# A two-layer decoder trunk: the instruction order worked out with the scheduler's timeline model in place of its default machine model

## The chip, the cores and the metric

The kernel runs on one core of a Trainium2 chip. The metric is the device time of one execution in microseconds (us); the time of a kernel is the median of its runs. The engines go by the names of the profile: PE (TensorE, matmuls), PEld (its weight loads), DVE (VectorE), ACT (ScalarE), POOL (GpSimd) and SP (SyncE, which issues the weight DMAs). Each engine works through its own list of instructions in the order in which they stand there, so the order decides which instruction stands behind which wait.

## The reference

256 tokens of 1024 features go through two layers. Cut to what matters here:

```python
x = x + mixer(rmsnorm(x))        # layer 0 ("even"): block attention (8 heads of 64) beside
                                 #   a Mamba-2 scan (16 heads), one input and one output projection
x = x + convffn(rmsnorm(x))      # 1024 -> 2816 gate and up, causal conv of width 3, 2816 -> 1024
x = x + ple(p[i], sigmoid(x))    # 256 -> 1024, gated
...                              # layer 1 ("odd"): the mixer is a gated DeltaNet, 16 value heads:
q, k, v = silu(causal_conv4(x @ w))
T = inv(I + strict_lower(beta * decay * k @ k.T))     # per head and chunk
o = norm(q @ state + intra_chunk(T, k, v)) * silu(z)  # z = x @ w_z
x = x + o @ w_out                # then the same FFN and per-layer embedding
```

Everything is float32.

## The kernel before, in words

**The matmul stream.** A float32 product is made of three matmuls on halves of 12 significant bits. `mm3` (L174) issues them for each of its k tiles at L181, L182 and L183; a tile over 1024 features is 8 k tiles, so 24 matmuls. This text calls one of these matmuls an mm3 instruction. The weights (about 140 MB) are streamed once, in blocks of 128 x 1024 by `piece` (L133): an SP DMA into one of 4 `raw` buffers, the high half `whi` on ACT (L155), the low half `wlo` on DVE (L156), into 4 buffers each. These two are placed at a priority 80 instructions ahead (L154).

**The layers.** `even` runs the attention and scan heads of layer 0 (decay rows through a DRAM round trip `rowdr` to the tile `AC`, L516, and the exponentials `E` from it, L529 to L532; the attention's sums of squares `sqk`, L563, and `pss`, L566). `ffn` and `ple` are long runs of mm3 work. `_odd` (L710) runs the DeltaNet over 8 head groups of two value heads. For each group there are

- `prep` (L785): two convolution tiles (`pgd`, 24 mm3 each), transposes `pkq` (L795), Gram matrices (L820, L821), and the inverse of four triangular 128 x 128 problems. That inverse is six levels, each `pY` on PE (L867), `zb` on DVE (L871), `pST` on PE (L875, L878), two copies on ACT; then two Newton steps, each `pR` on PE (L894 to L901), a copy on ACT (L903), `pC` on PE (L906), the update `S32` on DVE (L907).
- `vproj`: two `pgd` tiles for v and their transposes `pvT` (L920).
- `zproj` (L984): two tiles `pz` of 24 mm3 for the gate, whose results leave their bank on DVE (L991) into `z`, a tile of 4 buffers.
- `core` (L925): the chain `py0`, `pS1`, `pkS`, `X1` (DVE, L944), `py1`, `po`, then a norm of 13 small DVE instructions between ACT passes, and transposes `oT` (L981).
- `gate` (L996): reads `z`, writes the operands `gh` (L210) and `gl` (L211) of the output projection `w_out` (tiles `pwo`, L1005).

The loop at L1021 calls, for group kh: core(kh), gate(kh), prep(kh+2), vproj(kh+1), zproj(kh+2); `w_out` for the first half of the heads is called after the last group. PSUM banks of this phase: 3 shared by the `pgd`, `pz` and `pwo` tiles (chain `acc`), 1 for `core`, 2 and 1 for the two alternating `prep` chains.

**What sets the order.** The program above is only a list with priorities: earlier lines come first, the weight halves 80 ahead. The framework's scheduler plays the list in a simulated machine; whenever an engine of that machine is free, it takes the ready instruction of the highest priority, and the sequence of these choices becomes the order of each engine's list on the chip. Buffers are reused in the same rotation whatever the order. Which machine is simulated is set where the context is opened, at L1151.

Of the kernel before, what the change touches and what calls it, by code (L numbers as in the profile page):

```python
# [14 lines left out]
PSUM = bass.MemoryType.PSUM  # L15
# [16 lines left out]

# Columns of the packed per-feature vectors (feature on the partition).
PV = {}
# [6 lines left out]
NPV = _n  # L41
# Columns of the constants that depend on shapes alone.
CC = {}
# [7 lines left out]
class Trunk:  # L51
    def __init__(self, ctx, tc, stream, xT, pT, pv, tok, cst, out):
        self.tc, self.nc, self.ctx = tc, tc.nc, ctx
        self.stream, self.out = stream, out
        self.off = 0
        self.order = []
        self.n = 0
        self.pshare, self.share = 0.0, 0.0
        nc = self.nc
        ep = ctx.enter_context  # L60
        self.cpool = ep(tc.tile_pool(name="cpool", bufs=1))
        self.rawp = ep(tc.tile_pool(name="rawp", bufs=4))
        self.splp = ep(tc.tile_pool(name="splp", bufs=4))
        self.smallp = ep(tc.tile_pool(name="smallp", bufs=3))
        self.chain = ""
        self.nrm = ep(tc.tile_pool(name="nrm", bufs=1, space=PSUM))

        warm = self.cpool.tile([P, 1], F32, tag="warm", name="warm")
        nc.vector.memset(warm, 0.0)
        nc.scalar.activation(warm, warm, AF.Exp)  # L70
        # matmuls on zeros: TensorE's clock is up when the first operands arrive
        zt = self.cpool.tile([P, 256], F16, tag="zt", name="zt")
        nc.vector.memset(zt, 0.0)
        pz = self.nrm.tile([P, 512], F32, tag="nrm", name="pwarm")
        for _ in range(WARM):
            nc.tensor.matmul(pz[:, :T], zt[:, :P], zt, start=True, stop=True)
        self.pv = self.cpool.tile([P, NPV], F32, tag="pv", name="pv")
        nc.scalar.dma_start(self.pv, pv)
        xs = self.cpool.tile([P, KD, T], F32, tag="x", name="x")
        for m in range(0, KD, 2):  # L80
            nc.sync.dma_start(xs[:, m:m + 2], xT[:, m:m + 2])
        self.x = [xs[:, m] for m in range(KD)]
        self.tok = self.cpool.tile([P, 64], F32, tag="tok", name="tok")
        self.cst = self.cpool.tile([P, NCC], F32, tag="cst", name="cst")
        self.cst_src, self.tok_src = cst, tok
        self.pT = pT
        self.ones = self.cpool.tile([P, 1], F32, tag="ones", name="ones")
        nc.gpsimd.memset(self.ones, 1.0)
        self.ident = self.c("ident")
        self.id16 = self.cpool.tile([P, P], F16, tag="id16", name="id16")  # L90
        self.zb = [[self.cpool.tile([P, 4, P], F16, tag=f"zb{s}_{l}", name=f"zb{s}_{l}") for l in range(6)]
                   for s in range(1)]

# [1 line left out]
    def c(self, name):  # L95
# [11 lines left out]
    @contextmanager  # L107
    def psum(self, **banks):
        """The 8 PSUM banks of a phase, by the kind of work that rotates through them."""
        assert sum(banks.values()) <= 7  # L110
        with self.tc.tile_pool(name=self.uid("psum"), bufs=1, space=PSUM) as pool:
            self.psp, self.banks = pool, banks
            yield
# [12 lines left out]
    @contextmanager  # L126
    def on(self, chain):
        """Work of a chain of its own: its tiles don't wait for those of other chains."""
        was, self.chain = self.chain, chain
        yield  # L130
        self.chain = was

    def piece(self, blocks, lo=None):  # L133
        """Stream in weight blocks (array, layer, k0, nk, c0, nc), 1024 columns at a time, and split them."""
        nc = self.nc
        groups, g, cols = [], [], 0
        for b in blocks:
            n = b[3] * b[5]
# [27 lines left out]
    def lo_engine(self, share):  # L166
        """GpSimd takes a share of the low halves, VectorE the rest."""
        self.pshare += self.share if share is None else share
# [5 lines left out]
    def mm3(self, out, w, a, start=True, stop=True):  # L174
        """out += w.T @ a over k-tiles, w = (hi, lo) [128, nk, f], a = list of (hi, lo)."""
        nc = self.nc
# [26 lines left out]
    def split(self, src, hi, lo, scale=None):  # L203
        """hi + lo = src * scale, hi and lo of 12 significant bits."""
        nc = self.nc
# [7 lines left out]

# [1 line left out]
    def norm_begin(self, gain, pool=None):  # L215
# [42 lines left out]
    def replicate(self, r, n, dst=None):  # L258
        """[128 tok, n] -> [128, n*128] with row values on every partition."""
        nc = self.nc  # L260
# [7 lines left out]

# [1 line left out]
    def ffn(self, i, nxt):  # L270
# [38 lines left out]

# [1 line left out]
    def ple_proj(self, i, pool):  # L311
# [38 lines left out]

# [1 line left out]
    def conv4(self, pool, ps, w, b=None):  # L352
        """2 * silu(causal conv of R * ps), four taps, feature-major."""
        nc = self.nc
# [19 lines left out]
    def softplus(self, x, n, dst):  # L374
        """max(x, 0) + log1p(exp(-|x|)) on a [128, n] tile; log1p by its atanh series."""
        nc = self.nc
# [21 lines left out]
    def rowdram(self, col):  # L398
        """[128 tok, 32] -> [32, 128] in DRAM."""
        nc = self.nc  # L400
# [7 lines left out]

# [1 line left out]
    def even(self):  # L410
# [4 lines left out]
    def _even(self, mp):  # L415
# [5 lines left out]

        # dt, decay sums
        wdt, = self.piece([(W, 0, 0, KD, 4096, 16)])
# [42 lines left out]

        # B, C, x
        sw = lambda t: (lambda j: self.v("scw", t * 4 + j))
# [42 lines left out]
        def ssd(t):  # L511
            """heads 2t, 2t+1"""
            xf = feat[t]
# [26 lines left out]

        # q, k (feature-major), v (token-major)
        gqk = KEEP([P, 1], "gqk")
# [67 lines left out]

        # attention
        aA = []
# [42 lines left out]

        # z gate, group norm
        aS = []
# [29 lines left out]

        # output projection
        for m0 in (0, 4):
# [14 lines left out]

# [1 line left out]
    def odd(self):  # L706
# [3 lines left out]
    def _odd(self, mp):  # L710
# [16 lines left out]

        # beta, decay sums
        wab, = self.piece([(W, 0, 0, KD, 6144, 32)])
# [5 lines left out]
        for c in range(2):  # L735
            PE.transpose(ps[:, c * 32:(c + 1) * 32], abS[:, c * P:(c + 1) * P], ident[:32, :32])
        # softplus(a + dt_bias) and softplus(-b) = -log(sigmoid(b))
        ab = KEEP([P, 2, 32], "ab")
# [46 lines left out]
        def prep(kh):  # L785
# [17 lines left out]
            self.rsqrt(t, 4, rkq)  # L803
            # k stays as it is: 1 / |k| goes into the rows of the triangular system and its right sides,
            # and its solution times k needs none
            cs = TL([P, 3, 4], "cs", bufs=3)
# [8 lines left out]
            V.tensor_scalar(out=sq_, in0=rkq[:, 2:4], scalar1=128 ** -0.5, scalar2=None, op0=ALU.mult)  # L815
            # Gram matrices
            pk = self.sm("pkk")
# [7 lines left out]
            V.tensor_tensor(qk, pk[:, T:].rearrange("p (c t) -> p c t", c=2), bc(upper, 2), op=ALU.mult)  # L825
            # decays; index of a problem: chunk * 2 + head
            GC = KEEP([P, 4, P], "GC")
# [23 lines left out]
            Ll = TL([P, 4, P], "Ll", F16)  # L851
            # inverse of the unit triangular L by doubling its blocks; T16 = inv(L), S16 = its transpose
            T16 = TL([P, 4, P], "T16", F16)
# [34 lines left out]
            G.tensor_tensor(Ll, L32, L16, op=ALU.subtract)  # L888
            # two Newton steps in float32: S += S (I - L' S)
            S32 = TL([P, 4, P], "S32", bufs=3)  # L890
# [34 lines left out]
        def core(kh, st, bv):  # L925
            k2, qd, sq_, kt, Pm, S32, cs = st
            # chunk 0
            ps = self.sm("py0")
# [8 lines left out]
            A.activation(S1.rearrange("p e t -> p (e t)"), ps[:, :T], AF.Copy)  # L937
            # chunk 1
            ps = self.sm("pkS")
# [9 lines left out]
            A.activation(vn[1].rearrange("p e t -> p (e t)"), ps[:, :T], AF.Copy)  # L949
            # outputs, token-major, index of a problem: chunk * 2 + head  # L950
            po = self.sm("po")
            for e in range(2):
                PE.matmul(po[:, e * P:(e + 1) * P], Pm[:, e], vn[0][:, e], start=True, stop=True)
            for e in range(2):
                o = T + e * P
                PE.matmul(po[:, o:o + P], qd[:, e], S1[:, e], start=True, stop=False)
                PE.matmul(po[:, o:o + P], Pm[:, 2 + e], vn[1][:, e], start=False, stop=True)
            # normalisation over the value dim
            so = KEEP([P, 4, P], "so")
# [197 lines left out]
```

## Time and profile before

| | |
|---|---|
| median of 3 runs | 945.4 us (945.18 to 949.99) |
| profiled execution, span | 948.2 us |
| layer 0 mixer, 0 to 201 us | 201 us |
| layer 0 FFN and embedding, 201 to 417 us | 216 us |
| odd mixer, 417 to 730 us | 313 us |
| layer 1 FFN and embedding, 730 to 948 us | 218 us |

The profile is that of one execution, and its own time is its span of 948.2 us; no other time stands beside it. The stages are stretches of that span, with bounds where the tiles of one stage give way to those of the next. In each stretch the share of each engine's busy time shows which one has slack. Matmuls are pipelined and their ends are modelled, so the times between the starts of two PE instructions tell more than the busy time of one.

### The profile page before, as it was taken

What the parts mean: (1) busy time and instruction counts of PE and PEld (TensorE: products, weight loads), DVE (VectorE), ACT (ScalarE), POOL (GpSimd) and SP (SyncE); (2) the same over time, 40 slices, a digit from 0 to 9 for tenths busy, and PEclk for the clock granted to TensorE, in tenths of its full rate; (3) what the DMA queues carried; (4) which work ended last, traced back from release to release, by engine and by line L of the source; (5) the groups of instructions that cost most, each with busy time, mean ns of one, the idle gap of its engine ahead of it and who ended that gap; (6) DMA issues with size and microseconds to landing.
All of it is one profiled execution on the core that took longest, in us unless ns stands there. A gap on an engine that the chain in (4) does not pass through costs nothing.

```text
span 948.2 us, 19896 instructions
## 1 busy us (share of the span) xinstructions
PE 903.1 (95%) x7768; PEld 865.4 (91%) x7768; DVE 751.2 (79%) x1636; ACT 584.3 (62%) x1231; POOL 77.2 (8%) x83
## 2 busy tenths in 40 slices
PE   7979999999999999998989998999999999999998
PEld 5978778899999999987878898889899999999997
DVE  6767778888788766687889998999868888876665
ACT  5467656565655544664877777777745656654452
POOL 2000012110000001020111101111002000000100
PEclk9889999999999999999899999999999999999999
DMA  7544532456666555645333243322445555555562
GB/s 266 155 130 140 156 113 91 138 194 195 193 192 200 181 186 171 190 137 165 96 125 96 79 144 107 117 90 82 134 133 179 179 200 195 188 187 183 172 190 77
DMA packets 49822, 145.65 MB, mean 154 GB/s; under 512 B 9344, under 2 KB 15040, under 8 KB 49728
## 3 DMA queue, kind: packets, MB, share of 16 engines
q1 hardware_dynamic: 40608, 139.84, 46.7%
q10 hardware_dynamic: 9120, 4.53, 1.9%
q8 instruction: 61, 1.00, 0.4%
q14 instruction: 33, 0.27, 0.1%
HBM read 143.27 MB, written 1.08 MB: 152 GB/s over the span
## 4 chain that ended last, share of the span: by engine, by line
PE 75%; DVE 13%; DMA 4%; ACT 4%; issue 2%; POOL 1%; ACTq 0%; SPq 0%; POOLq 0%
PE pd L181 4%; PE pd L183 4%; PE pd L182 4%; PE pg L181 4%; PE pg L182 4%; PE pu L181 4%; PE pu L182 4%; PE pg L183 4%; PE pu L183 4%; DVE wlo L156 4%; DMA AC<-rowdr 2%; DMA GC<-rowdr 2%; PE pwo L182 2%; PE pgd L183 2%; PE pgd L181 2%
## 5 line engine op out<-in xcount | busy, mean ns | idle before, releaser
L156 DVE TENSOR_TENSOR wlo<-raw,whi 128x1024 fp32r<-128x1024 f32 (+2 forms) x266 | 323.5, 1217 | 89.1 <-ACT whi L155 85.6
L155 ACT ACTIVATE whi<-raw 128x1024 fp32r<-128x1024 f32 (+2 forms) x266 | 276.3, 1039 | 173.3 <-PE pd L182 46.3
L183 PE MATMUL pd<-yh,wlo 128*128 128x256 f32 x352 | 99.6, 283 | 0.0
L181 PE MATMUL pd<-yh,whi 128*128 128x256 f32 x352 | 99.6, 283 | 0.0
L182 PE MATMUL pd<-yl,whi 128*128 128x256 f32 x352 | 99.6, 283 | 0.0
L181 PE MATMUL pg<-xh,whi 128*128 128x256 f32 x352 | 97.3, 277 | 0.6 <-DVE x L1011 0.3
L181 PE MATMUL pu<-xh,whi 128*128 128x256 f32 x352 | 97.3, 277 | 0.0
L182 PE MATMUL pg<-xl,whi 128*128 128x256 f32 x352 | 97.3, 277 | 0.0
L183 PE MATMUL pg<-xh,wlo 128*128 128x256 f32 x352 | 97.2, 276 | 0.0
L182 PE MATMUL pu<-xl,whi 128*128 128x256 f32 x352 | 97.2, 276 | 0.0
L183 PE MATMUL pu<-xh,wlo 128*128 128x256 f32 x352 | 97.2, 276 | 0.0
L181 PE MATMUL pgd<-xh,whi 128*128 128x256 f32 x256 | 76.3, 298 | 0.3 <-DVE z L991 0.3
L182 PE MATMUL pgd<-xl,whi 128*128 128x256 f32 x256 | 74.9, 293 | 0.0
L183 PE MATMUL pgd<-xh,wlo 128*128 128x256 f32 x256 | 74.8, 292 | 0.0
L363 DVE SCALAR_TENSOR_TENSOR chh<-cg,pv,chh 128x255 f32<-128x255 f32 x132 | 66.7, 505 | 4.0 <-ACT chh L361 2.1
L183 PEld LDWEIGHTS pd<-yh,wlo 128*128 128x128 f32 x352 | 67.6, 192 | 0.0
L181 PEld LDWEIGHTS pd<-yh,whi 128*128 128x128 f32 x352 | 67.6, 192 | 0.0
L182 PEld LDWEIGHTS pd<-yl,whi 128*128 128x128 f32 x352 | 67.6, 192 | 0.0
L181 PEld LDWEIGHTS pg<-xh,whi 128*128 128x128 f32 x352 | 66.1, 188 | 0.8 <-issue 0.8
L182 PEld LDWEIGHTS pu<-xl,whi 128*128 128x128 f32 x352 | 66.1, 188 | 0.0
L183 PEld LDWEIGHTS pu<-xh,wlo 128*128 128x128 f32 x352 | 66.1, 188 | 0.0
L182 PEld LDWEIGHTS pg<-xl,whi 128*128 128x128 f32 x352 | 66.1, 188 | 0.0
(358 smaller groups left out, 2657.5 us busy)
## 6 DMA issues: line engine op xcount, KB each, us to landing
raw<-stream SPq DMA_DIRECT2D x232, 512.0 KB, 3.6
raw<-stream SPq DMA_DIRECT2D x32, 448.0 KB, 3.2
AC<-rowdr ACTq DMA_DIRECT2D x16, 128.0 KB, 4.0
GC<-rowdr ACTq DMA_DIRECT2D x16, 128.0 KB, 4.0
x<-xT SPq DMA_DIRECT2D x4, 256.0 KB, 5.0
out<-x SPq DMA_DIRECT2D x8, 128.0 KB, 1.8
cst<-cst SPq DMA_DIRECT2D x1, 645.0 KB, 6.4
raw<-pT SPq DMA_DIRECT2D x2, 256.0 KB, 2.5
```

Of the source, the lines that this page charges most:

```text
L155: nc.scalar.activation(hi[:, :cols], raw[:, :cols], AF.Copy)
L156: self.lo_engine(lo).tensor_tensor(lo_[:, :cols], raw[:, :cols], hi[:, :cols].bitcast(F32), op=ALU.subtract)
L181: nc.tensor.matmul(out, wh, ah, start=start and k == 0, stop=False)
L182: nc.tensor.matmul(out, wh, al, start=False, stop=False)
L183: nc.tensor.matmul(out, wl, ah, start=False, stop=stop and k == n - 1)
L363: nc.vector.scalar_tensor_tensor(out=h[:, s:], in0=g[:, :T - s], scalar=w(3 - s), in1=h[:, s:], op0=ALU.mult, op1=ALU.add)
```

## The change

The context is opened with the scheduler's timeline model as the simulated machine. Comments and docstrings were dropped as well; the line numbers stay.

```diff
-    with tile.TileContext(nc) as tc:
+    with tile.TileContext(nc, schedule_with_timeline_sim=True) as tc:
         order = tile_trunk(tc, **aps, out=out)
```

Both programs hold the same instructions on the same buffers on every engine. Only the order on each engine differs. Three places show how.

**ACT, layer 0, the first decay rows.** `E` needs `AC` from DRAM; `sqk` is what `pss` on PE waits for. Before:

```order
L516 DMA AC_158_741<-rowdr_88_335 128x256 x2
L516 DMA AC_164_767<-rowdr_88_335 128x256
L361 ACTIVATE chh_120_555<-cg_119_553,pv_106 128x256
L155 ACTIVATE whi_174_801<-raw_173_799 128x1024
L529 ACTIVATE E_162_750<-AC_158_741,ac_84_329 128x128
L530 ACTIVATE E_162_750<-AC_158_741,cross_90_339 128x128
L531 ACTIVATE E_162_750<-AC_158_741,ac_84_329 128x128
L529 ACTIVATE E_163_758<-AC_158_741,ac_84_329 128x128
L532 ACTIVATE E_162_750<-E_162_750 128x384
L560 ACTIVATE kT0_153_704<-pqk_152_679,gqk_128_580 128x256
L370 ACTIVATE cth_122_561<-chh_120_555 128x256
L563 ACTIVATE sqk_154_706<-pqk_152_679 128x256
```

With the change:

```order
L404 ACTIVATE rowsb_86_333<-rowps_85_331 32x128
L406 DMA rowdr_88_335<-rowsb_86_333 32x128
L560 ACTIVATE kT0_153_704<-pqk_152_679,gqk_128_580 128x256
L563 ACTIVATE sqk_154_706<-pqk_152_679 128x256
L155 ACTIVATE whi_187_879<-raw_186_877 128x1024
L370 ACTIVATE cth_122_561<-chh_120_555 128x256
L502 ACTIVATE gm0_124_567<-pG_123_564 128x128
L361 ACTIVATE chh_138_622<-cg_137_620,pv_106 128x256
L459 DMA last_89_337<-rowdr_88_335 128x16x1
L516 DMA AC_158_741<-rowdr_88_335 128x256 x2
L516 DMA AC_164_767<-rowdr_88_335 128x256 x2
```

The two instructions of the attention, L560 and L563, moved from behind the first five `E` instructions to a place ahead of the DMA that loads `AC`.

**DVE, odd mixer, the inversions of the first two head groups.** The `zb` tiles are one level each; `pY_1229` and `pY_1231` belong to group 0, `pY_1306`, `pY_1308`, `pY_1310` and `pY_1312` to group 1. Before, around the fourth and fifth level of group 0:

```order
L871 TENSOR_TENSOR zb0_3_121<-pY_1229_5903,cst_114 128x16x16
L198 TENSOR_TENSOR rt_1285_6176<-rt_1284_6175,st_1277_6162 128x4
L371 SCALAR_TENSOR_TENSOR v2_1342_6454<-cth_1346_6487,chh_1345_6482 128x256
L199 SCALAR_TENSOR_TENSOR ry_1286_6177<-rt_1285_6176,ry_1283_6171 128x4
L363 SCALAR_TENSOR_TENSOR chh_1351_6523<-cg_1350_6521,pv_106,chh_1351_6523 128x255
L197 SCALAR_TENSOR_TENSOR rt_1287_6181<-ry_1286_6177 128x4
L156 TENSOR_TENSOR wlo_1457_6930<-raw_1455_6927,whi_1456_6929 128x1024
L871 TENSOR_TENSOR zb0_4_122<-pY_1231_5920,cst_114 128x8x32
```

With the change:

```order
L871 TENSOR_TENSOR zb0_1_119<-pY_1306_6249,cst_114 128x64x4
L871 TENSOR_TENSOR zb0_3_121<-pY_1229_5903,cst_114 128x16x16
L871 TENSOR_TENSOR zb0_2_120<-pY_1308_6266,cst_114 128x32x8
L871 TENSOR_TENSOR zb0_4_122<-pY_1231_5920,cst_114 128x8x32
L871 TENSOR_TENSOR zb0_3_121<-pY_1310_6283,cst_114 128x16x16
L871 TENSOR_TENSOR zb0_5_123<-pY_1233_5937,cst_114 128x4x64
L871 TENSOR_TENSOR zb0_4_122<-pY_1312_6300,cst_114 128x8x32
L907 SCALAR_TENSOR_TENSOR S32_1235_5956<-pC_1238_5969,S16_1221_5845 128x512
```

Between two levels of group 0 stood convolution, rsqrt and weight work for other tiles; now levels of the two groups stand next to each other, with nothing between them. On PE, from `pY_1227` to the transposes of core 0, no mm3 instruction stands any more.

**PE, odd mixer, the core of the last head group.** Before, with `pwo` the output projection of the first eight heads:

```order
L930 MATMUL py0_2197_10062<-bv_2184_9979,S32_2108_9684 128x128 x2
L181 MATMUL pwo_2244_10247<-gh3_1516_7173,whi_2241_10217 128x256
L182 MATMUL pwo_2244_10247<-gl3_1517_7174,whi_2241_10217 128x256
L183 MATMUL pwo_2244_10247<-gh3_1516_7173,wlo_2242_10218 128x256
L181 MATMUL pwo_2244_10247<-gh4_1646_7726,whi_2241_10217 128x256
L935 MATMUL pS1_2200_10068<-vn0_2198_10065,kt_2064_9495 128x128 x2
L182 MATMUL pwo_2244_10247<-gl4_1647_7727,whi_2241_10217 128x256
L183 MATMUL pwo_2244_10247<-gh4_1646_7726,wlo_2242_10218 128x256
L181 MATMUL pwo_2244_10247<-gh5_1648_7731,whi_2241_10217 128x256
L182 MATMUL pwo_2244_10247<-gl5_1649_7732,whi_2241_10217 128x256
L940 MATMUL pkS_2202_10073<-S1_2201_10071,k2_2052_9421 128x256
```

With the change:

```order
L930 MATMUL py0_2197_10062<-bv_2184_9979,S32_2108_9684 128x128 x2
L935 MATMUL pS1_2200_10068<-vn0_2198_10065,kt_2064_9495 128x128 x2
L940 MATMUL pkS_2202_10073<-S1_2201_10071,k2_2052_9421 128x256
L948 MATMUL py1_2204_10078<-X1_2203_10075,S32_2108_9684 128x128 x2
L953 MATMUL po_2205_10082<-vn0_2198_10065,Pm_2089_9554 128x128 x2
L956 MATMUL po_2205_10082<-S1_2201_10071,qd_2090_9555 128x128
L957 MATMUL po_2205_10082<-vn1_2199_10066,Pm_2089_9554 128x128
L956 MATMUL po_2205_10082<-S1_2201_10071,qd_2090_9555 128x128
L957 MATMUL po_2205_10082<-vn1_2199_10066,Pm_2089_9554 128x128
L981 MATMUL oT_2224_10130<-cst_114,on_2223_10125 128x128 x4
L181 MATMUL pwo_2267_10413<-gh14_2225_10136,whi_2262_10403 128x256
```

The core's steps now stand one behind the other, and the mm3 instructions of the first half of `w_out` stand ahead of them. Only tiles that still need this group's own `gh14`, or that come after them, are left behind it.

## Rows read from the trace of the kernel before

**Rows 1.** The page, part 1: busy time, share of the span, instructions.

```profile
PE 903.1 (95%) x7768; PEld 865.4 (91%) x7768; DVE 751.2 (79%) x1636; ACT 584.3 (62%) x1231; POOL 77.2 (8%) x83
```

**Rows 2.** Windows by stage: busy time per engine, granted clock, DMA share, GB/s.

```profile
core 0: us, PE busy (x) PEld busy (x) DVE busy (x) ACT busy (x) POOL busy (x), PEclk, DMA share, GB/s
...
201.00:417.00 216.00, 214.18 (x1843) 213.83 (x1844) 163.81 (x266) 123.29 (x194) 9.95 (x11) 1.00 0.59 185
417.00:730.00 313.00, 291.75 (x2767) 276.02 (x2768) 272.65 (x752) 222.72 (x599) 37.27 (x31) 0.98 0.39 118
500.00:670.00 170.00, 160.00 (x1576) 150.39 (x1574) 157.81 (x455) 129.26 (x361) 22.08 (x17) 1.00 0.35 106
730.00:948.00 218.00, 213.57 (x1838) 213.19 (x1837) 158.72 (x259) 115.43 (x177) 5.63 (x6) 1.00 0.55 175
250.00:300.00 50.00, 50.00 (x443) 50.00 (x443) 40.80 (x65) 29.16 (x47) 0.00 (x0) 1.00 0.60 196
```

**Rows 3.** Timeline of PE at 52.6: start, duration, instruction, idle time before it.

```profile
52.66 0.80 PE L566 MATMUL pss<-cst,sqk 128*128 128x2 f32 x3 [5.37 <-ACT sqk L563]
```

**Rows 4.** Timeline of ACT from 50.2 to 52.5.

```profile
50.28 0.40 ACT L530 ACTIVATE E<-AC,cross 128x128 f32<-128x128 f32 x1 [2.29 <-DMA AC<-rowdr]
...
52.25 0.36 ACT L563 ACTIVATE sqk<-pqk 128x256 f32<-128x256 f32 x1
```

**Rows 5.** Timeline of PE at 451.7.

```profile
451.73 0.48 PE L795 MATMUL pkq<-cst,k 128*128 128x128 f32 x1 [5.78 <-DVE k L371]
```

**Rows 6.** Windows, the stretches of half granted clock after those waits and at 486.

```profile
52.60:59.40 6.80, 6.74 (x29) 6.56 (x30) 4.34 (x11) 4.03 (x10) 0.00 (x0) 0.50 0.06 19
448.60:455.40 6.80, 3.67 (x17) 3.68 (x18) 4.16 (x14) 4.95 (x16) 2.00 (x2) 0.50 0.35 112
486.10:489.50 3.40, 3.40 (x23) 2.99 (x23) 0.71 (x4) 2.44 (x9) 0.00 (x0) 0.50 0.43 147
```

**Rows 7.** Window of the odd layer, the matmuls of line L181 alone.

```profile
417.00:730.00 313.00, 152.82 (x522) 99.29 (x523) 0.98 0.39 118
```

**Rows 8.** Timeline of PE, one level of an inversion.

```profile
491.64 0.28 PE L867 MATMUL pY<-S,L 128*128 128x64 f16 x4
...
492.53 0.29 PE L875 MATMUL pST<-zb,T 128*128 128x64 f16 x4
...
492.77 0.33 PE L795 MATMUL pkq<-cst,q 128*128 128x128 f32 x1
...
493.74 0.28 PE L867 MATMUL pY<-S,L 128*128 128x64 f16 x4
```

**Rows 9.** Timeline of PE, the Newton steps of one head group.

```profile
499.46 0.22 PE L898 MATMUL pR<-S,L 128*128 128x128 f16 x1
...
502.21 1.05 PE L901 MATMUL pR<-S,L 128*128 128x128 f32 x8
...
504.23 0.28 PE L906 MATMUL pC<-R,T 128*128 128x128 f16 x2
```

**Rows 10.** Timeline of PE, the core of the last head group.

```profile
686.41 0.40 PE L906 MATMUL pC<-R,T 128*128 128x128 f16 x4
...
692.80 0.70 PE L953 MATMUL po<-vn,Pm 128*128 128x128 f32 x4
...
701.26 0.66 PE L981 MATMUL oT<-cst,on 128*128 128x128 f32 x4
```

**Rows 11.** Timeline of DVE, the end of the last gate.

```profile
703.01 0.87 DVE L211 SCALAR_TENSOR_TENSOR gl<-z,nh,gh 128x256 fp32r<-128x256 f32 x2
```

**Rows 12.** Groups of DVE in the odd layer, by form: busy, mean ns, idle before.

```profile
L156 DVE TENSOR_TENSOR wlo<-raw,whi 128x1024 fp32r<-128x1024 f32 x66 | 84.1, 1275 | 7.6 <-ACT whi L155 6.2 <-ACT T L881 1.3
L871 DVE TENSOR_TENSOR zb<-pY,cst 128x256 f16<-128x256 f32 x48 | 20.1, 419 | 7.6 <-PE pY L867 7.5
```

## The prediction

> **What bounds the kernel now.** Start with the page's busy times: PE 903.1 us of 948.2, DVE 751.2 [rows 1]. PE looks full, but its busy time is stretched where it waits inside a stream, so the stages come next. In both FFN stages PE is full by any reading: 50 us hold 443 recorded instructions, 0.113 us each, and DVE has slack (163.81 of 216, 158.72 of 218) [rows 2]. The changed program has nearly the same order there, so I cost these 434 us at nothing; the cover is PE's full list, behind which DVE and ACT work ahead. If a weight half came late there, each block would show at most its 1.28 us on DVE [rows 12].
>
> The odd mixer is different. PE is issued 522 x 3 recorded mm3, at 0.113 us 177 us [rows 7, 2], and its small matmuls. Per head group I estimate those at 9.4 us: a level shows 0.24 us for two of its three sets of four matmuls (492.53 to 492.77), so six levels come to 2.2 [rows 8]; the Newton steps about 2.1, of which one float32 set is 1.05 [rows 9]; core and transposes 5, from sets of 0.66 and 0.70 [rows 10]. Eight groups give 75, so PE needs about 252 of 313 us. DVE is busy for 272.65, and in the steady part, 500 to 670, for 157.81 of 170 while PE shows 160.00 [rows 2]. So neither engine alone sets the end here; two engines, each above 90%, feed each other, and the price of this is 170 / 157.81, a factor of 1.08 over the busier one. What keeps it so low is that the long dependent chains of the inversion run under mm3 work.
>
> In layer 0 the trace shows one large wait: PE stands for 5.37 us before pss, which needs sqk from ACT [rows 3]. ACT had stood behind E, whose AC came from DRAM, for 2.29 us with sqk queued after it [rows 4]. Just behind that wait the granted clock is 0.50, the 1.2 GHz level, for 6.8 us; the same stands around the wait of 5.78 us for pkq at the start of the odd mixer [rows 5, 6].
>
> **The change, step by step.** It removes and adds no instruction, DMA or buffer. All that can change is which wait stands ahead of what.
>
> *Layer 0.* The order puts sqk ahead of the DMA of AC, so the wait of 5.37 us should go, and with it half of the 6.8 us at half clock, 3.4: together -8.8. Against this: at the start ACT squares the residual between the splits, which delays the first operands (estimate +2); the last group norm's rep comes later (+1.5); and with the z tiles used up earlier, the attention pairs have only 9 mm3 instructions each between their hops (+3). These three are estimates without a row of their own; each lies between 0 and 6, the largest wait that any hop of this trace shows [rows 5]. Sum -2, bounds -9 and +8.
>
> *The odd mixer.* Here the order changes its kind. Before, a dependent chain was spread with 3 to 10 mm3 instructions between hops. Now there are fill stretches with 18 to 24 between hops, and seven stretches with none, because the three acc banks are held: a pz waits for a z buffer (4 of them), z is free only when gate has read it, and gate stands at the end of that chain. PE's list then holds nothing but the chain, and all mm3 work stands behind it.
>
> Prices of an uncovered chain: a level 2.10 us (pY 491.64 to the next pY 493.74) [rows 8]; both Newton steps 4.77 (499.46 to 504.23) [rows 9]; a core from pC to po 6.39 (686.41 to 692.80), po to oT 8.46, of which two weight halves that lay between on DVE are 2.55, and oT to the end of the gate 2.6 (701.26 to 703.88): together 14.9 [rows 10 to 12]. The first inversions run from pY_1227 to the first gate bare: four levels of group 0 8.4, Newton 4.8, core and gate 14.9, 28.1 in all, with group 1 running in their shadow. The others, in program order: 1.5 levels 3.2; 3.5 levels, half a Newton and a gate 12.4; Newton and three levels 11.1; three levels 6.3; Newton and four levels, two of them half hidden, 13.2; at the end half a Newton and the last core 17.3. Sum 91.6, bounds 78 (the DVE work of the seven stretches, counted by kind at the mean durations of before, is 69, and nine hand-overs of 1 us are not hidden) and 105 (each hop a seventh longer, behind other work in DVE's list).
>
> PE's own work in those stretches is about 40 of its 252 us, so 212 remain outside, and DVE has 272.65 - 69 = 204 left. With the factor 1.08 the rest takes 212 x 1.08 = 229; bounds 213 (no wait at all) and 240. Before, the chain's 92 us lay beside this work; now they are added to it, and the rest gets shorter by less than that. The wait for pkq at the start goes, since about 60 mm3 instructions now stand ahead of it; it is part of the 313 and not of the 229.
>
> *The clock.* A stretch at 0.50 costs half its length: 3.4 us for those of 6.8, 1.7 for that of 3.4 at 486 [rows 6]. Two follow waits of over 5 us; the bare hops have idle times of about 1 us, but dozens in a row with few matmuls. I take three of seven stretches at 3.4, +10; bounds 0 and 24 (all seven).
>
> The Trainium skill, page "TensorE: Matmul & The Clock Gate", section "HAM oscillation — how this bites in real kernels", says that idle gaps between bursts of matmuls drop the clock to half rate again and again; the two stretches of 6.8 us agree, since each stands around a wait. By that rule all seven stretches would fall, 24 would stand where I take 10, and the time would be 975; the last rival below is its harder form.
>
> *Sum.* Odd mixer 91.6 + 229 + 10 = 331 for 313, +18. Layer 0 -2. Profiled span 948.2 + 16 = 964. The median of the runs shown is 2.8 below this span, so the forecast is **961 us**. With the bounds of the terms taken as independent, the case's own range is 948 to 977.
>
> **The rivals.** *Hops overlap, faster.* If the bare stretches take their lower bound, 78, and the rest runs at PE's own 213 with 5 for the clock, the odd mixer takes 296, 17 less; with layer 0 at -5 the time is 948.2 - 22 - 2.8 = 923. For it: two groups' levels stand side by side in the first stretch, so one group's hop hides the other's, and with wider fill between hops DVE would work off its list without interruption. Against it: only the first stretch has two whole problems; DVE shows zb waiting 7.5 us in all for pY now, little to win [rows 12]. It decides where bare and rest together stay below 313.
>
> *A wash.* Bare 85, rest 222 and clock 5 make 312, layer 0 -2: 942 to 946, no change that can be told. It needs a rest better packed than the steady part before, at a factor of 1.05.
>
> *The clock stays down, slower still.* If the engine runs at 0.50 through every bare stretch and into the fill behind it, 24 stands for 10, and about 12 of the chain's own 40 us of PE work are added: 948.2 + 42 - 2.8 = 987. For it speak the rows at 0.50 [rows 6]; against it, that 500 to 670 shows a mean clock of 1.00 with a similar density of small hops, though with mm3 work between them [rows 2].
>
> That the order on the chip would not be the one of the program is no rival: each engine's list is fixed.
>
> **How the numbers follow.** A difference under 0.5% (4.7 us) is about what a measurement of this kernel cannot tell from none. The forecast has a chance of 0.56 (0.52 of it slower by more than that, 0.04 within), the clock 0.14, the wash 0.13 (0.09 within, 0.02 to either side), the faster rival 0.17. So faster 0.19, same 0.13, slower 0.68. The range of 8 in 10 runs from 934 to 984: about a tenth, the better part of the faster rival, lies below, and under a tenth, the worst of the clock rival, above.
>
> **What the profile after would show.** Right: no wait of over 2 us before pss; seven stretches in the odd mixer where PE shows only small matmuls with idle times near 1 us before each, the longest about 28 us near the first core and 17 before the rest of w_out; the odd mixer at 320 to 345 us with DVE's busy time still near 273, so its share falls; clock of 0.50 in some of these stretches. Wrong in the faster direction: the odd mixer below 313 and levels in the bare stretches nearer to 1.6 us than to 2.1. Wrong in the slower one: clock of 0.50 in most of the seven, or the fill stretches no tighter than 1.08 over the busier engine. Another way to be wrong is the FFN stages: if either leaves 216 or 218 us by more than 2, the weights arrive otherwise than I read from the order.

## The result and the profile after

The changed kernel takes 1023.3 us (median of 4 runs, 1018.4 to 1030.0) where the kernel before takes 947.7: a ratio of 1.080, 95% interval 1.074 to 1.086. It is slower, as forecast, but by 76 us and not by 16, and outside the range of 934 to 984.

The page of the profiled execution, part 1:

```profile
PE 921.5 (91%) x7768; PEld 880.2 (87%) x7768; DVE 761.0 (75%) x1636; ACT 587.3 (58%) x1231; POOL 75.1 (7%) x83
```

PE is busy for 18 us more than before [rows 1] although it does the same work; its share fell from 95% to 91%. The windows show where: the granted clock of the odd mixer is 0.89.

Windows by stage (columns as in [rows 2]), and then the stretches of the odd mixer in which PE runs no mm3 instruction for more than 6 us:

```profile
202.00:420.00 218.00, 215.82 (x1844) 215.67 (x1845) 162.30 (x266) 123.55 (x194) 9.74 (x11) 0.99 0.59 183
420.00:799.00 379.00, 311.15 (x2769) 292.14 (x2768) 284.29 (x753) 226.93 (x599) 35.56 (x32) 0.89 0.32 97
799.00:1016.00 217.00, 213.12 (x1836) 212.91 (x1835) 157.28 (x259) 115.31 (x177) 5.63 (x6) 1.00 0.57 175
472.10:480.60 8.50, 1.16 (x9) 0.65 (x8) 7.69 (x22) 6.31 (x16) 3.30 (x3) 0.77 0.55 163
494.40:533.40 39.00, 25.07 (x236) 20.52 (x234) 20.04 (x63) 19.82 (x65) 2.65 (x2) 0.71 0.11 35
558.40:565.40 7.00, 2.26 (x27) 1.43 (x23) 7.00 (x21) 4.95 (x12) 1.54 (x2) 0.76 0.41 131
589.90:608.30 18.40, 9.38 (x99) 7.81 (x97) 12.82 (x51) 12.08 (x41) 2.68 (x2) 0.76 0.15 49
631.30:647.90 16.60, 11.03 (x93) 9.24 (x92) 12.80 (x47) 10.48 (x33) 2.66 (x2) 0.68 0.24 77
671.80:679.10 7.30, 2.45 (x35) 1.82 (x33) 6.89 (x20) 4.72 (x13) 2.62 (x2) 0.93 0.44 117
703.60:721.70 18.10, 12.87 (x134) 10.59 (x132) 15.02 (x56) 11.97 (x40) 2.68 (x2) 0.93 0.18 57
760.50:777.80 17.30, 7.36 (x46) 5.39 (x44) 4.35 (x19) 4.56 (x18) 0.00 (x0) 0.88 0.00 0
```

The stages have the bounds of [rows 2], moved to where the same tiles now stand. The odd mixer takes 379 us, 66 more than its 313. The FFN of layer 0 takes 2 more, the last stage 1 less, and what is left, 1 us, is layer 0's mixer (202 for 201). So 66 of the 68 us between the two spans lie in the odd mixer. The eight stretches, the lower rows, make 132.2 us of it; PE is busy in 71.6 us of them, at granted clocks of 0.68 to 0.93 where the stage before has 0.98.

What PE waits for in the odd mixer (us in total, times, longest):

```profile
PE pS L858 <- DVE T L854: 14.4, 4, 6.8
PE pST L875 <- DVE zb L871: 12.1, 13, 2.8
PE oT L981 <- ACT on L977: 10.2, 4, 5.2
PE pY L867 <- ACT T L881: 7.1, 9, 2.7
```

Before, the first two were these, and the third and fourth under 1 us each; they are the steps of the chain.

```profile
PE pS L858 <- DVE T L854: 6.7, 7, 1.6
PE pST L875 <- DVE zb L871: 0.6, 1, 0.6
```

One more table is worked out from the starts of PE's instructions, from the first small step behind the stage's first rep to the last oT. A step is a group of small matmuls of one line (the two lines of pST count as one); its time runs to the start of the next step, and the mm3 instructions between the two are counted (at 0.113 us each where their time is given).

| | steps with none behind | with 1 to 11 | with 12 and more | all, less mm3 time |
|---|---|---|---|---|
| before | 211: 53.0 us | 163: 145.0 us | 17: 78.0 us | 131 us |
| after | 289: 146.3 us | 30: 26.7 us | 57: 169.4 us | 193 us |

A step with no mm3 instruction behind it is called bare. Before, a bare step takes 0.25 us on the mean; after, 0.51 us, and there are more of them. The first column grows by 93 us; the other two, less their mm3 time, give back 31 of these, which leaves the 62.

### The profile page after: what moved, and what is told of

Read it like the earlier page. It is cut to its first block, busy times and chain, and to the rows that moved or that the text cites. A ratio compares the mean times of both kernels' runs of the same rounds, so it can differ in the third digit from the quotient of the medians.

```text
span 1016.6 us, 19947 instructions
## 1 busy us (share of the span) xinstructions
PE 921.5 (91%) x7768; PEld 880.2 (87%) x7768; DVE 761.0 (75%) x1636; ACT 587.3 (58%) x1231; POOL 75.1 (7%) x83
## 4 chain that ended last, share of the span: by engine, by line
PE 76%; DVE 10%; ACT 6%; DMA 4%; issue 2%; ACTq 0%; DVEq 0%
PE pd L181 4%; PE pd L183 4%; PE pd L182 4%; PE pg L181 4%; PE pg L182 4%; PE pu L181 4%; PE pg L183 4%; PE pu L182 4%; PE pu L183 4%; PE pgd L181 3%; PE pgd L182 3%; PE pgd L183 3%; DMA GC<-rowdr 3%; DVE wlo L156 2%; PE pz L181 2%
## 5 line engine op out<-in xcount | busy, mean ns | idle before, releaser
L181 PE MATMUL pd<-yh,whi 128*128 128x256 f32 x352 | 99.3, 283 | 0.0
L181 PE MATMUL pg<-xh,whi 128*128 128x256 f32 x352 | 97.9, 278 | 0.6 <-DVE x L701 0.3
L181 PE MATMUL pu<-xh,whi 128*128 128x256 f32 x352 | 97.6, 277 | 0.0
L181 PE MATMUL pgd<-xh,whi 128*128 128x256 f32 x256 | 77.8, 304 | 3.2 <-DVE cg L356 2.0
L181 PEld LDWEIGHTS pd<-yh,whi 128*128 128x128 f32 x352 | 67.4, 192 | 0.0
L181 PEld LDWEIGHTS pg<-xh,whi 128*128 128x128 f32 x352 | 66.4, 189 | 0.8 <-issue 0.8
L183 PEld LDWEIGHTS pg<-xh,wlo 128*128 128x128 f32 x352 | 66.5, 189 | 0.0
L181 PEld LDWEIGHTS pu<-xh,whi 128*128 128x128 f32 x352 | 66.4, 189 | 0.0
```

Of the source, the lines that this page charges most:

```text
L181: nc.tensor.matmul(out, wh, ah, start=start and k == 0, stop=False)
L183: nc.tensor.matmul(out, wl, ah, start=False, stop=stop and k == n - 1)
```

## The experiments

Six theories are told apart. **A, spacing**: PE's new order puts 18 to 24 mm3 instructions between two hops, and later none, so the hops of the chain stand bare. **B, banks**: the z buffers hold the acc banks and keep mm3 work out of the bare stretches (the prediction's mechanism). **C, decays**: ACT waits for the single GC buffer. **D, clock**: the bare stretches pull the clock down, and this is the cost. **E, the lists of ACT and DVE** make the loss, not that of PE. **G, sequence**: which steps of the chains stand next to each other makes it, not the mm3 work between. Each run was timed beside the kernel before; ratios are to that. Wherever the program or PE's order is changed, the scheduler works out the lists of the other engines anew, so no run moves one list alone.

**Six z buffers** (t_z6), a test of B.

```diff
-                z = TL([P, T], "z", bufs=4)
+                z = TL([P, T], "z", bufs=6)
```

The diff is cut: it leaves out that `psq` goes from two buffers to one to make room, here and in the other runs with six z or two GC buffers.

> The changed kernel with 6 z buffers in the odd mixer in place of 4 (and one psq buffer in place of 2, to make room). Theory A, the fill runs out: the new order spends 18 to 24 mm3 instructions on each hop of the chain until none is left, whatever the buffers are; by the order 128 hops of the odd mixer stand in bare stretches instead of 138, so 1005 to 1022 us. Theory B, the banks (that of the prediction): z buffers hold the acc banks, and with two more of them mm3 work gets between the hops: below 985 us.

Measured: 1005.8 us, ratio 1.064 (1.058 to 1.070). The odd mixer, and its longest bare stretch:

```profile
423.00:784.00 361.00, 304.93 (x2765) 286.72 (x2766) 281.89 (x754) 223.54 (x600) 37.05 (x32) 0.91 0.35 102
520.10:550.40 30.30, 21.12 (x175) 17.42 (x174) 23.91 (x85) 19.10 (x67) 4.83 (x4) 0.81 0.14 37
```

The longest bare stretch shrank from 39.0 to 30.3 us and the odd mixer from 379 to 361. Seven stretches of over 6 us are left, 112.5 us for the eight of 132.2. So the z buffers, and the new order that the model makes with them (over 1000 of PE's 7768 instructions stand out of the change's sequence), give back 17.5 of 76 us: B has a part, and below 985 us, as it was expected to bring, is not reached. More than six z buffers were not tried.

**Two GC buffers** (t_gc2), a test of C.

```diff
-            GC = KEEP([P, 4, P], "GC")
+            GC = TL([P, 4, P], "GC")
```

> The changed kernel with two GC buffers in place of one (and one psq buffer). Theory C, the decay rows: the two waits of 6.8 us before pS and the waits of ACT for GC come from the single GC buffer, whose next load starts only when the last reader of the group before has run: they go, and the time is 1000 to 1010 us. Rival (A alone): the order still has 138 bare hops, the freed time is waited out elsewhere: 1013 to 1025 us.

Measured: 1019.5 us, ratio 1.078 (1.071 to 1.085): no change. ACT no longer shows a wait for GC among its longest, yet PE's list of waits begins with the same line:

```profile
PE pS L858 <- DVE T L854: 12.3, 3, 5.6
```

So the long waits for pS are not made by that DMA alone. In the program it is one link of a chain (pkq, squares, rsqrt, scaled rows, POOL, ACT, DVE, pS); no run takes that chain apart.

**More work in the bare hops** (t_warm), a test of D.

```diff
                 o = CC["zm"][0] + l * 64
+                [PE.matmul(py[:, T:512], id16, T16[:, 0:2], start=True, stop=True)
+                 for _ in range(6 if kh * 6 + l in BARE else 0)]
```

> The changed kernel with six more matmuls of 256 columns behind pY in 29 of the 48 levels, those that stand in bare stretches; they write into the half of pY's bank that nobody reads, so the result is the same and PE has 174 x 0.107 = 18.6 us more to do. Theory D, the clock: PE idles in the bare hops, the granted clock falls to 0.50 there and stays down in the fill behind. With more work in the hops the half-clock time of the odd mixer (85 us) falls below 50, and the time falls to 1000 to 1012 us in spite of the added work. Rival: the clock follows something else, the half-clock time stays, and the time is 1018 to 1035 us.

Measured: 1027.0 us, ratio 1.086 (1.080 to 1.092). The odd mixer, and the longest bare stretch:

```profile
423.00:804.00 381.00, 319.22 (x2939) 298.38 (x2940) 286.12 (x756) 226.99 (x602) 36.26 (x32) 0.93 0.32 96
501.70:540.50 38.80, 27.74 (x312) 22.60 (x310) 20.55 (x64) 20.98 (x68) 2.65 (x2) 0.91 0.10 33
```

The clock rose: 0.93 for 0.89 over the stage, which is 2 x 0.07 x 381 = 53 us at 0.50 where the change has 2 x 0.11 x 379 = 83, and 0.91 for 0.71 in the longest stretch. Yet that stretch takes 38.8 us for 39.0, and the time did not fall. Had all 18.6 us of added work lain on the path, the 30 us fewer at 0.50 would have been worth 18.6 - 3.6 = 15 us, half of their length; had none, nothing. The rows say that some of it lay there. In the longest stretch, with the added matmuls at L868:

```profile
506.67 0.28 PE L867 MATMUL pY<-S,L 128*128 128x64 f16 x4
...
507.56 0.82 PE L868 MATMUL pY<-T,id 128*128 128x256 f16 x6
508.21 0.28 PE L875 MATMUL pST<-zb,T 128*128 128x64 f16 x4
...
509.42 0.28 PE L867 MATMUL pY<-S,L 128*128 128x64 f16 x4
```

No idle time stands before pST: it comes right behind the added work, and the level takes 2.75 us. Three such levels (503.75 to 512.16) take 8.4 us, where the change (496.50 to 503.02) took 6.5. The stretch as a whole got no longer, so the rest of it gained about 2 us, with 2 x 0.09 x 38.8 = 7 us at 0.50 for 2 x 0.29 x 39.0 = 23. So D is not refuted: by these rows, of one execution each, the low clock has a price of its own. How much of the 76 us it is, this run does not tell, since its added work took back what the clock gave.

**Two GC buffers in the kernel before** (d_gc2).

> The kernel before (default machine model) with two GC buffers and one psq buffer. Theory C holds for any order in so far as ACT waits for GC: 5.1 us of such waits in the odd mixer before go, and 43 instead of 55 hops stand bare: 938 to 943 us. Rival: PE works through those waits, no change, 944 to 950 us.

Measured: 949.3 us, ratio 1.001 (0.999 to 1.004). No change: the rival.

**PE's order by itself** (d_peT, and t_peD as its mirror image), A against E. After the program is traced, the instructions of one engine are chained in a given order, with edges that set the order of issue and add no wait:

```diff
-        order = tile_trunk(tc, **aps, out=out)
+        order = tile_trunk(tc, **aps, out=out); impose(nc, tc)
```

> The default machine model, with PE held to the order that the timeline model gave it (each PE instruction is queued behind the one that stood before it there; no waits are added); ACT, DVE, POOL and SP are ordered by the default model around that. Theory A, PE's order spends the mm3 work early and leaves hops bare, whatever the other engines do: 1005 to 1030 us. Rival E, the lists of ACT and DVE do it, in which the decays of a later group stand ahead of the norm of an earlier one: 950 to 975 us.

Measured: 1030.5 us, ratio 1.086 (1.079 to 1.093). PE's order is enough to make the whole loss, with every other engine ordered by the default model around it:

```profile
424.00:809.00 385.00, 311.90 (x2757) 293.73 (x2756) 283.78 (x750) 225.76 (x596) 35.32 (x31) 0.88 0.31 94
```

Those lists follow PE's: by the starts in the traces, at least 568 of 1636 DVE instructions stand out of the sequence that they have in the kernel before, and 380 out of that of the change.

> The mirror image: the timeline model, with PE held to the order of the kernel before. Theory A: 942 to 956 us. Rival E: 995 to 1020 us.

Measured: 997.1 us, ratio 1.051 (1.043 to 1.059):

```profile
424.00:767.00 343.00, 302.08 (x2780) 283.65 (x2779) 279.54 (x758) 224.08 (x602) 36.81 (x32) 0.97 0.36 108
```

This missed theory A's 942 to 956 and lies at the lower edge of E's range. The odd mixer takes 343 us; bare steps are as short as before (210 of them, 51.6 us), and the loss stands in the 163 steps with 1 to 11 mm3 instructions, 167.8 us for 145.0. So the lists of ACT, DVE and the rest can cost time too, where they are made around an order of PE that the model would not have chosen. Of its 48 us, 30 lie in the odd mixer. The two halves don't add up (81 and 48 us, 76 together), so this is no second term of the same sum.

**Spacing in the changed order** (t_spread5, t_slack8). PE keeps the changed order, only the mm3 instructions between hops are thinned out and put later.

> The changed kernel with PE held to its own order but for the mm3 instructions of the odd mixer: they keep their sequence, yet only 5 go between two hops of the chain, and the rest waits until data needs it or a later hop has room. By the order 97 hops of the odd mixer stand in bare stretches of at least four, where the change has 138 and the kernel before 55. Theory A: from 947 and 1023 us at 55 and 138 hops, 0.92 us a hop, so 985 us, 975 to 1000. Rival: the sequence of the chains among themselves, which is kept, makes the loss, not the spacing of the mm3 work: 1010 to 1030 us.

Measured: 1066.5 us, ratio 1.125 (1.117 to 1.134), worse than both theories. It is spoilt by its own edit: PE stood idle for 32.9 us, in seven waits, for the v tiles ahead of their transposes pvT, a wait that its list does not show with the change. The next version keeps every tile 20 hops ahead of its use.

> The changed kernel with PE held to its own order but for the spacing: 8 mm3 instructions between two hops where 18 to 24 stood, and each tile done at least 20 hops before data needs it (the earlier version with 5 let the v tiles come just before their transposes). 117 bare hops where the change has 138. Theory A: 995 to 1012 us. Rival G: 1015 to 1035 us, since the sequence of the chains is kept.

Measured: 1023.5 us, ratio 1.082 (1.078 to 1.087), as the change itself. By the table's count, 119 steps now have 1 to 11 mm3 instructions, and 242 stand bare at 132.5 us, where the change has 289 at 146.3; all steps less mm3 time are 195 us for 193. Thinning the fill did not help here, with the bare stretches still there; this falls into G's range and outside A's.

**Spacing in the order before** (d_block), A against G. PE keeps the order of the kernel before, with the 24 mm3 instructions of each tile of the odd mixer put together where the last of them stood.

> The kernel before with PE held to its own order but for one thing: in the odd mixer the 24 mm3 instructions of a tile stand together, at the place of the last of them, so every tile is done where it was done before, the sequence of the chains is the same, and only the spacing changes: 205 hops stand in bare stretches of at least four where before 55 do. Theory A, spacing: what lies between two hops of a chain is what hides them, so 990 us or more (0.92 us a hop, from 55 and 138 hops at 947 and 1023 us, would give 1085 at most). Rival G, sequence: which steps of the chains stand next to each other makes the loss, not where the mm3 work lies between them: 944 to 962 us.

Measured: 1031.9 us, ratio 1.088 (1.083 to 1.094). The odd mixer, and what PE waits for in it:

```profile
416.00:807.00 391.00, 312.89 (x2744) 290.90 (x2741) 276.69 (x747) 225.40 (x594) 36.84 (x30) 0.93 0.31 92
```

```profile
PE pST L875 <- DVE zb L871: 14.2, 20, 1.7
PE pC L906 <- ACT R L903: 8.0, 9, 1.8
```

344 steps stand bare, 171.5 us, and 45 with 18 and more. On PE no chain moved against another, and the kernel lost as much as with the change, with the granted clock at 0.93. So G falls as the only cause: spacing is enough by itself, as far as PE's list goes.

One reservation stands. The default model worked out the lists of DVE and ACT around the new order of PE: by the starts in the traces, at least 270 of 1636 DVE and 182 of 1269 ACT entries stand out of the sequence of the kernel before. Two runs speak against these lists as the cause. d_gc2 has as many out of sequence (272 and 212) and lost nothing; and t_peD, whose loss is one of lists, has its bare steps as short as before, where here the loss stands in the bare steps. A run with all lists held was not made. And whether the sequence of the chains has a part in the changed kernel's loss, as t_slack8 suggests, stays open.

**E behind sqk in the kernel before** (d_sqk2), one term of the prediction by itself.

```diff
-                A.activation(sq, ps[:, :T], AF.Square)
+                self.after = A.activation(sq, ps[:, :T], AF.Square).ins
+                ia = self.tc.issue_after(self.after); ia.__enter__()
                 A.activation(E[:, 0], AC[:, 0, e], AF.Relu, scale=-1.0, bias=ac[:, h:h + 1])
...
                 A.activation(E, E, AF.Exp, scale=-1.0)
+                ia.__exit__(None, None, None)
```

> The kernel before with one edit in layer 0: on ACT the E instructions of a pair of scan tiles are queued behind the sqk of the same pass, as the timeline model ordered them. The prediction's -8.8 us by itself (the wait of 5.4 us for pss and half of the 6.8 us at half clock behind it): 936 to 941 us. Rival: E comes later and PE waits for it instead: 945 to 954 us.

Measured: 945.6 us, ratio 0.998 (0.995 to 1.001). PE's longest wait in the first 200 us is now one of 2.0 us; the wait for pss is gone from its list. In the profile the FFN of layer 0 starts (first pg on PE) at 194.3 us, where the three traces that left layer 0 alone show 197.2 to 200.9; the whole time gains 2 us, with an interval from a gain of 4.4 to a loss of 0.5, so it is not clear of none. The wait went as predicted; that it was worth 8.8 us is not borne out.

**Layer 0 of the change by itself** (d_evenT): the default model, with the mixer of layer 0 held to the new order on every engine.

> The default machine model, with the instructions of the layer 0 mixer alone held to the order of the timeline model, on every engine; the rest is as in the kernel before. The prediction's term for layer 0 is -2 us, so 943 to 946. By the profile after, the wait for sqk went, but waits for weight halves behind E came in its place, 203 us for 201: 947 to 951.

Measured: 956.3 us, ratio 1.008 (1.004 to 1.012). It costs 7 us, above both expectations. The kept traces say the same: the seven whose layer 0 has the new order on every engine start its FFN at 202.2 to 208.1 us, the three with the old order at 197.2 to 200.9.

**Both edits in the kernel before** (d_sqk_z6).

> The kernel before with E queued behind sqk in layer 0, and 6 z buffers (one psq buffer) in the odd mixer. If z buffers hold mm3 work back from bare hops under any order, as the 17 us that they gave back to the changed kernel suggest, some of it shows here too: 936 to 943 us. Rival: under the default model the hops are covered already, 943 to 949 us.

Measured: 942.3 us over 12 runs, ratio 0.995 (0.993 to 0.998). It is the fastest version found, about half a per cent ahead of the kernel before. Its interval reaches into both expectations, and six z buffers by themselves were not run in this kernel, so which edit gives it is not shown.

## Why the prediction was wrong

**The direction and the place** held: the odd mixer, bare stretches in front of the gates, and a fill that had been spent. d_peT shows PE's order as the cause, and d_block that spacing is enough to lose as much. The reason given for the bare stretches, z buffers that hold the banks, is worth 17.5 of the 76 us with two more of them.

**The step that failed is the price of the uncovered chain**, 91.6 us with bounds of 78 and 105. The seven stretches it named take 123.7 us, and an eighth that it did not name, before the first pS, takes 8.5:

| stretch | 1 | 2 | 3 | 4 | 5 | 6 | 7 |
|---|---|---|---|---|---|---|---|
| forecast, us | 28.1 | 3.2 | 12.4 | 11.1 | 6.3 | 13.2 | 17.3 |
| measured, us | 39.0 | 7.0 | 18.4 | 16.6 | 7.3 | 18.1 | 17.3 |

The last one, with a core alone on every list, came out. So the prices were right for a chain that has the lists to itself, and wrong where steps of several groups stand in them. A level held only while two groups' levels went in step. PE in the longest stretch:

```profile
498.76 0.55 PE L867 MATMUL pY<-S,L 128*128 128x64 f16 x8 [0.48 <-ACT T L881]
...
500.75 0.65 PE L867 MATMUL pY<-S,L 128*128 128x64 f16 x8 [0.48 <-ACT T L881]
...
503.02 0.37 PE L867 MATMUL pY<-S,L 128*128 128x64 f16 x4 [0.17 <-ACT T L881]
```

From pY to pY 1.99 and 2.27 us, for both groups, against 2.10. In the second stretch the hop from pY to pST by itself takes 3.07 us. PE, then DVE:

```profile
560.27 0.28 PE L867 MATMUL pY<-S,L 128*128 128x64 f16 x4 [0.53 <-ACT S L879]
563.34 0.37 PE L875 MATMUL pST<-zb,T 128*128 128x64 f16 x4 [2.79 <-DVE zb L871]
```

```profile
560.61 1.22 DVE L156 TENSOR_TENSOR wlo<-raw,whi 128x1024 fp32r<-128x1024 f32 x1
...
561.82 1.13 DVE L846 SCALAR_TENSOR_TENSOR L<-Dn,cs,kk 128x128 f32<-128x128 f32 x4
562.87 0.42 DVE L871 TENSOR_TENSOR zb<-pY,cst 128x256 f16<-128x256 f32 x1
```

A weight half and the decays of another group stand ahead of zb in DVE's list. The bound of 105 had each hop a seventh longer for such work; the six stretches together are 106.4 us for 74.3, longer by over two fifths.

The largest miss is the core of the first stretch, and with it the phrase that group 1 runs in the shadow of group 0: steps of groups 1 and 2 stand between those of group 0. The end of that stretch on PE:

```profile
509.48 0.58 PE L906 MATMUL pC<-R,T 128*128 128x128 f16 x4 [0.53 <-ACT R L903]
...
511.86 0.64 PE L820 MATMUL pkk<-k 128*128 128x128 f32 x2
...
518.99 0.71 PE L953 MATMUL po<-vn,Pm 128*128 128x128 f32 x4
...
527.30 0.61 PE L858 MATMUL pS<-id,T 128*128 128x128 f16 x4 [6.70 <-DVE T L854]
529.89 1.12 PE L981 MATMUL oT<-cst,on 128*128 128x128 f32 x4 [1.99 <-ACT on L977]
...
533.38 0.56 PE L181 MATMUL pgd<-xh,whi 128*128 128x256 f32 x1
533.74 0.41 PE L182 MATMUL pgd<-xl,whi 128*128 128x256 f32 x1
533.95 0.41 PE L183 MATMUL pgd<-xh,wlo 128*128 128x256 f32 x1
```

From the last pC of group 0 to po 9.5 us for 6.4, with the Gram matrices pkk of group 2 and Newton steps of group 1 between; from po to oT 10.9 for 5.9, with pS of group 2 between, which waits 6.70 us; from oT to the first mm3 3.5 for 2.6. ACT in the same stretch:

```profile
520.86 0.33 ACTq L830 DMA_DIRECT2D GC<-rowdr  x1
...
524.68 0.69 ACT L841 ACTIVATE Dn<-GC,ngc 128x128 f32<-128x128 f32 x2 [2.82 <-DMA GC<-rowdr]
...
528.70 1.14 ACT L977 ACTIVATE on<-po,st 128x128 f32<-128x128 f32 x4 [1.40 <-DVE st L973]
```

and DVE:

```profile
522.09 1.27 DVE L970 TENSOR_SCALAR st<-st 128x4 f32<-128x4 f32 x1
...
526.82 0.42 DVE L854 TENSOR_TENSOR T<-L,sm 128x512 f16<-128x512 f16 x1 [1.67 <-ACT L L850]
527.16 1.11 DVE L198 TENSOR_TENSOR rt<-rt,st 128x4 f32<-128x4 f32 x1
...
528.50 0.16 DVE L973 TENSOR_TENSOR st<-ry,sqs 128x4 f32<-128x4 f32 x1
```

Group 0's norm is in this list too: its L198 stands behind T (L854) of group 2, which waits 1.67 us for ACT, and ACT waits for GC until 524.7. Whichever group is latest, the others wait with it.

**The clock** was to cost 10, with 24 for all seven stretches. The stage shows 83 us at 0.50 where it had 6.8 and 3.4 [rows 6]. 57 of them lie in the eight stretches and the rest in the fill behind them, where mm3 instructions follow each other at 0.21 us (533.74 to 533.95) for 0.113; half of that rest, some 13 us, is an estimate of what the clock costs in the fill. In the stretches its price is not known: the rows of t_warm speak for more than nothing, and leave it open. The Trainium skill, page "TensorE: Matmul & The Clock Gate", section "HAM oscillation — how this bites in real kernels", says that gaps between bursts put the clock back each time; the granted clock of 0.68 to 0.93 in all eight stretches agrees.

**The rest of the odd mixer** was forecast at 229 and 10 for the clock; outside the eight stretches it takes 379 - 132 = 247. This term was off by 8 us.

**Two sums do not come out as written.** Both Newton steps and four levels, two of them half hidden, are 4.77 + 2 x 2.10 + 2 x 1.05 = 11.1 by the prediction's own prices, not 13.2. And its bounds, taken as independent (the root of the sum of their squares), reach from about 937 to 985, not from 948 to 977. Neither makes up for the miss.

**Layer 0** was to gain 2. It lost 1 between the two profiles, but about 7 by d_evenT, and the other traces agree with the 7. The wait for pss went as forecast, but ACT, freed from E there, meets it later. ACT:

```profile
54.50 0.40 ACT L529 ACTIVATE E<-AC,ac 128x128 f32<-128x128 f32 x1 [1.92 <-DMA AC<-rowdr]
...
64.03 1.04 ACT L155 ACTIVATE whi<-raw 128x1024 fp32r<-128x1024 f32 x1
```

The weight half at 64.0 stands behind the twelve E instructions that start at 54.50 and, by the same timeline, three other weight halves and four DMA issues of AC, and PE waits for it, 2.76 us:

```profile
65.14 0.36 PE L181 MATMUL pqk<-xh,whi 128*128 128x256 f32 x1 [2.76 <-ACT whi L155]
```

**What stays open**: how the loss divides between bare hops and the clock that stands at 0.50 in them, whether the sequence of the chains adds to it, and why the timeline model's lists for ACT and DVE cost 48 us around PE's old order (t_peD).

## What to carry to other kernels

Where two engines are both over 90% busy, a new order is judged by what stands between the hops of the dependent chains: count the steps with no independent work behind them. Moving the same matmuls from the gaps into blocks cost 85 of 947 us here, with the sequence of the chains on PE kept and the other lists worked out around it. A bare chain must be priced with every other chain's steps that stand in the same lists, and a wait that is removed is worth only the distance to the next limit: here some 2 us, not clear of none, of the 8.8 that the wait and the clock behind it had seemed to cost.

## What the runs showed of the hardware that was not expected

A DVE instruction on 128 x 4 values, L970, 0.17 us on the mean before, took 1.27 us (above, at 522.09) while a POOL instruction ran for the same time:

```profile
522.08 1.26 POOL L848 TENSOR_TENSOR L<-L,cst 128x512 f32<-128x512 f32 x1 [33.55 <-DVE st L967]
```

L198 at 527.16 took 1.11 us beside the next one of POOL (526.86, 1.39 us). The fourteen kept traces bear it out for all DVE instructions on 128 x 4 values of the rsqrt and norm lines: those that run beside no POOL instruction take at most 0.173 us, over 180 in each trace, and every longer one, up to 1.27 us, runs beside one. With the change there are ten of these, 8.3 us more than at 0.167 each, where before there are two. The one at 527.16 stands between pS and oT above; the one at 522.09 is followed by a wait of DVE for ACT that is longer than it. That POOL causes it was not tried by a run.
